# One token block of four taken alone through every mixer in plain float32, and two blocks instead of one served by gathered expert rows

## The chip, the cores and the metric

One core of a Trainium2 chip runs the whole kernel. The metric is the time of one execution on the device, in microseconds. Inputs and weights start in DRAM, the result ends there.

## What is computed

One layer over 512 tokens of 1024 channels, in float32. From the reference, cut:

```python
h = rmsnorm(x, norm_mix_g)
cb, cc, cx, q, k, v, gc, ga = split(h @ w_in)            # eight times 1024 columns
y_conv = (cb * causal_conv3(cc * cx)) @ w_conv_out
y_attn = diff_attention(q, k, v) @ w_attn_out            # 8 heads, causal, relative bias
x = x + (sigmoid(gc) * y_conv + sigmoid(ga) * y_attn) @ w_mix_out
x = x + cross_attention(rmsnorm(x), rmsnorm(mem))        # 256 memory positions, 4 heads
hf = rmsnorm(x)
# 8 heads each choose 16 of 16384 experts by two lists of 128 keys
act = gelu(einsum('td,thkd->thk', hf, peer_u[experts]))
x = x + einsum('thk,thkd->td', softmax(top_s) * act, peer_v[experts])
return rmsnorm(x, final_g)
```

## The kernel before

A block is 128 tokens. Up to the experts all four blocks (T = 512 columns) go together, channels on the partitions. A weight chunk of 1024 x 128 comes by one DMA of 512 KB on SP's queue (`weight`, line 106) and is split into two float32r parts, `hi` on ScalarE (line 98) and `lo` on VectorE (line 99), three buffers each. `product` (line 114) then makes 24 TensorE products: eight pieces of 128 channels, three passes each (hi by hi, hi by lo, lo by hi), 512 columns wide. There are 64 chunks of `w_in`, 8 each of four other mixers' weights and of `w_cq`, 16 of `w_pq`, and 16 of `w_ckv` (256 memory columns).

Order of the program: the memory's keys and values and the input's norm; eight heads of attention (`diff_head`), each beside one of eight convolution channels; the gates and the output projections; cross-attention; the queries and the choice of experts (`keys_scores`, `keys_pairs`); the experts. A scheduler orders each engine's instructions from this program; each engine then works in its own order.

The bias by distance is made once: `parameters` (line 192) lays a small table out and writes it, one copy per partition, to the DRAM tile `toep` by one DMA of 2560 KB from eight partitions; each head reads its part from there.

The experts are handled in two ways. Blocks 1 to 3 (TY = 384 columns, "dense") go against all experts: `stage_u` (line 687) multiplies 128 experts' chunk of `uT` with the dense tokens and applies gelu, 128 times; `gates` (line 823) lays the gates out densely with one-hot products, eight one-hot rows for four tokens; then for each of 128 chunks of `peer_v` 18 products of 512 columns sum up (line 750), six PSUM banks. The first 96 chunks of `uT` come before the first of `peer_v`, the other 32 beside them.

Block 0 is gathered: `gathered` (line 774) fetches, for step s below 128, one row of `peer_u` for each token by an indirect DMA issued by GpSimd, and VectorE multiplies it with the token's normed row and sums (line 801); for steps from 128 the same with `peer_v`, where VectorE adds the row times its weight to an accumulator (line 812). These 256 steps lie beside the dense work, from the choice of experts on. An index column is copied first (line 798).

The lines that the steps below touch most often:

```python
118             xhi, xlo = x[0][k], x[1][k]
119             for p, (ww, xx) in enumerate(((whi, xhi), (whi, xlo), (wlo, xhi))):
120                 self.nc.tensor.matmul(out, ww[:, k, :], xx, start=(k == 0 and p == 0), stop=(k == KC - 1 and p == 2))
...
801                     nc.vector.tensor_tensor_reduce(out=t, in0=t, in1=hx, op0=ALU.mult, op1=ALU.add, scale=1.0, scalar=0.0, accum_out=wx[:, 0, s : s + 1])
...
812                         nc.vector.scalar_tensor_tensor(out=acc, in0=t, scalar=w, in1=acc, op0=ALU.mult, op1=ALU.add)
...
818                 nc.gpsimd.indirect_dma_start(out=t, out_offset=None, in_=a["peer_u"] if s < P else a["peer_v"],
819                                              in_offset=bass.IndirectOffsetOnAxis(ap=idx, axis=0))
```

Of the kernel before, what the change touches and what calls it, by code (L numbers as in the profile page):

```python
# [32 lines left out]
NY = 3  # L33
# [11 lines left out]
SOON = 5  # memory weights loaded ahead of the input  # L45
# [6 lines left out]
MM = 1  # gate banks taken from the products  # L52
X_HEAD = 4  # gathered rows by two heads' choice
X_BLOCK = 3  # and by each block of tokens' gates
XW = 3  # rows in a step with an activation, to one in a step without
LAST = 2  # steps without rows at the end
LAST_J = 2  # blocks summed up token block by token block at the end
GRP = 8
TB = 24


class Block:
    # tag: (pool, slots)
    TAGS = {
# [22 lines left out]
    def ps(self, tag, shape=(P, 512)):  # L87
        self.count += 1
        return self.psum.tile(list(shape), F32, tag="ps" + tag, name=f"ps{tag}_{self.count}", bufs={"mm": 3, "lg": 2, "tr": 2, "pv": 1}[tag])

    def rows(self, name):
# [9 lines left out]
    def split_new(self, tag, src, n=T):  # L101
        hi, lo = self.t(tag, [P, n], F32R), self.t(tag, [P, n], F32R)
        self.split(hi, lo, src)
        return hi, lo

    def weight(self, dram_ap):
        raw = self.t("raw", [P, KC, P])
        self.nc.sync.dma_start(out=raw, in_=dram_ap)
        hi = self.t("hi", [P, KC, P], F32R)
        lo = self.t("lo", [P, KC, P], F32R)  # L110
        self.split(hi, lo, raw)
        return hi, lo

    def product(self, out, w, x):
        """out[c, t] = sum over d of w[d, c] x[d, t]"""
# [6 lines left out]
    def project(self, w, x, n=T):  # L122
        out = self.ps("mm")[:, :n]
        self.product(out, self.weight(w), x)
        return out

# [11 lines left out]
    def roots(self, out, acc, n, inv, eps, log=False, bank="tr"):  # L138
        """out[t, i] = 1 / sqrt(inv * sum of squares + eps) of token 128 i + t; acc holds sums by partition"""
# [26 lines left out]
    def spread(self, r, n, bank="tr"):  # L166
        """the tokens' values along the free dim, on every partition (in PSUM)"""
# [7 lines left out]
    def setup(self):  # L175
# [12 lines left out]
        m = self.misc = c("misc", [P, 48])  # L188
# [3 lines left out]
    def parameters(self):  # L192
        nc, a, m = self.nc, self.a, self.misc
        nc.vector.tensor_scalar(out=self.g_sub, in0=self.small[:, 56:57], scalar1=1.0 - LAM_INIT, scalar2=None, op0=ALU.mult)
        # lambda = exp(q1.k1) - exp(q2.k2) + init, the same on every partition
        lam = self.t("aw", [P, 4, 64])
        src = a["lam"]
        nc.gpsimd.dma_start(out=lam, in_=bass.AP(tensor=src.tensor, offset=src.offset, ap=[[0, P], [64, 4], [1, 64]]))
        for i in range(2):
            junk = self.t("aw", [P, 64])  # L200
# [4 lines left out]
        # relative bias by distance, reversed: entry e stands for distance 511 - e  # L205
        rb = self.t("vt", [32, H])
# [3 lines left out]
        oneh = [self.t("rs", [32, half]) for _ in range(2)]  # L210
        for i in range(2):
            nc.gpsimd.dma_start(out=oneh[i], in_=a["buckets"][:, i * half : (i + 1) * half])
        tab = self.t("aw", [H, TAB])
# [8 lines left out]
    def norm_of(self, x):  # L222
        acc = None
        for k in range(KC):
            acc = self.add_square(acc, x[k], T)
        r = self.misc[:, 8:12]
# [710 lines left out]
```

## Time and profile before

| what | value |
|---|---|
| median of 3 runs | 2156.46 us (2150.41 to 2160.2) |
| profiled execution, span | 2152.3 us |
| TensorE (PE) busy | 2048.0 us, 95% |
| VectorE (DVE) busy | 1505.0 us, 70% |
| ScalarE (ACT) busy | 1004.1 us, 47% |
| GpSimd (POOL) busy | 341.4 us, 16% |
| moved by DMA | 440.09 MB, mean 204 GB/s |

The profiled execution lies 4 us under the median and inside the range of the runs; its span is what the sums below are made against. PE, DVE, ACT, POOL and SP are the engines' names in the profile; PEld is TensorE's loading of weights. Products overlap in the profile (each lasts longer than the distance to the next one), so a rate is read from the distance between starts, not from the mean of one.

### The profile page before, as it was taken

The numbers are of one execution on the slowest core, as the hardware profiler recorded it, in microseconds if no ns is written. First come the engines' busy times: TensorE is split into PE (matmuls) and PEld (weight loads), VectorE is DVE, ScalarE is ACT, GpSimd is POOL, SyncE is SP. The second block draws the span as 40 slices with busy tenths as digits, with TensorE's granted clock in tenths as the row PEclk, the third lists the DMA queues.
The fourth block names the chain that finished last, engine by engine and source line by source line (L and its number), as shares of the span: only waits on it lengthen the run. The fifth ranks groups of instructions, "written<-read, shape, count | busy, mean of one in ns | idle before, by whom it ended". The sixth has DMA issues, their size and how long they took to land.

```text
span 2152.3 us, 29167 instructions
## 1 busy us (share of the span) xinstructions
PE 2048.0 (95%) x10341; PEld 1772.6 (82%) x10341; DVE 1505.0 (70%) x3531; ACT 1004.1 (47%) x1716; POOL 341.4 (16%) x301
## 2 busy tenths in 40 slices
PE   7499999999999999999998999999999999999997
PEld 6477877788887878899898989988777877888985
DVE  5356565642345568999887777557887887887897
ACT  5244444432233344343369999953333333333332
POOL 1000000000000000001231111012222234564431
PEclk9799999999999999999999999999999999999999
DMA  7532222223433124246687777589999988899984
GB/s 219 135 98 74 74 85 78 69 88 98 145 110 100 60 78 127 87 129 219 206 281 273 266 279 244 194 299 307 350 321 333 340 310 276 312 357 352 350 298 157
DMA packets 162787, 440.09 MB, mean 204 GB/s; under 512 B 15185, under 2 KB 70497, under 8 KB 160593
## 3 DMA queue, kind: packets, MB, share of 16 engines
q1 hardware_dynamic: 124464, 300.98, 41.7%
q0 software_dynamic: 38176, 137.25, 18.6%
q8 instruction: 81, 1.33, 0.2%
q14 instruction: 66, 0.53, 0.1%
HBM read 391.50 MB, written 46.66 MB: 204 GB/s over the span
## 4 chain that ended last, share of the span: by engine, by line
PE 51%; DMA 13%; DVE 13%; ACT 12%; issue 7%; POOL 2%; another core or an unknown queue 2%; SPq 0%; ACTq 0%; DVEq 0%; POOLq 0%
PE psmm L120 30%; PE psmm L750 5%; ACT slot L858 5%; PE pslg L120 5%; PE pstr L750 4%; DVE lo L99 3%; DMA raw<-in_peer_v 3%; DMA res<-in_peer_v,e 3%; ACT sq L850 3%; DMA act<-sp 2%; ACT hi L98 2%; PE pspv L750 2%; DMA res<-in_peer_u,e 1%; DMA res<-in_peer_u,kp 1%
## 5 line engine op out<-in xcount | busy, mean ns | idle before, releaser
L98 ACT ACTIVATE hi<-raw 128x1024 fp32r<-128x1024 f32 x388 | 410.9, 1061 | 633.0 <-PE psmm L120 288.4
L99 DVE TENSOR_TENSOR lo<-raw,hi 128x1024 fp32r<-128x1024 f32 x388 | 472.7, 1220 | 302.4 <-ACT hi L98 296.1
L120 PE MATMUL psmm<-A,hi 128*128 128x512 f32 x1408 | 451.1, 397 | 1.9 <-DVE Yb L450 1.9
L120 PE MATMUL psmm<-n,hi 128*128 128x384 f32 x1472 | 391.4, 343 | 1.2 <-ACT sp L695 1.2
L120 PEld LDWEIGHTS psmm<-A,hi 128*128 128x128 f32 x1408 | 262.3, 188 | 60.0 <-issue 4.2
L120 PE MATMUL psmm<-A,lo 128*128 128x512 f32 x704 | 280.6, 399 | 0.0
L120 PEld LDWEIGHTS psmm<-n,hi 128*128 128x128 f32 x1472 | 266.7, 188 | 1.6 <-ACT sp L695 1.5
L120 PE MATMUL psmm<-n,lo 128*128 128x384 f32 x736 | 251.6, 342 | 4.7 <-DVE lo L99 4.5
L818 POOL DMA_INDIRECT res<-in_peer_u,e x85 | 94.1, 1107 | 453.9 <-DVE e L798 430.2
L120 PEld LDWEIGHTS psmm<-A,lo 128*128 128x128 f32 x704 | 132.7, 189 | 28.6 <-issue 2.0
L98 ACT ACTIVATE tr<-e 128x384 fp32r<-128x384 f32 x128 | 66.6, 520 | 182.9 <-DVE e L739 179.0
L120 PE MATMUL pslg<-n,hi 128*128 128x384 f32 x576 | 148.3, 338 | 0.0
L120 PEld LDWEIGHTS psmm<-n,lo 128*128 128x128 f32 x736 | 138.3, 188 | 8.2 <-DVE lo L99 7.9
L750 PE MATMUL psmm<-hi,tr 128*128 128x512 f32 x384 | 129.0, 400 | 15.5 <-ACT tr L98 8.5
L801 DVE CUSTOM_DVE_ANT_0 res<-res,hx 128x1024 f32<-128x1024 f32 x101 | 122.5, 1219 | 24.8 <-DMA res<-in_peer_u,e 16.9
L750 PE MATMUL psmm<-lo,tr 128*128 128x512 f32 x384 | 131.1, 396 | 0.3 <-DVE lo L99 0.3
L818 POOL DMA_INDIRECT res<-in_peer_v,e x74 | 103.7, 1401 | 125.2 <-DVE e L808 103.1
L750 PE MATMUL psmm<-hi,e 128*128 128x512 f32 x384 | 119.6, 397 | 1.7 <-DVE e L798 1.6
L818 POOL DMA_INDIRECT res<-in_peer_u,kp x16 | 20.4, 1274 | 616.5 <-DVE kp L798 552.7
L120 PEld LDWEIGHTS pslg<-n,hi 128*128 128x128 f32 x576 | 105.3, 188 | 3.1
L856 DVE TENSOR_SCALAR oh<-iota,e 128x128 f32<-128x128 f32 x384 | 106.8, 345 | 0.0
L812 DVE SCALAR_TENSOR_TENSOR acc<-res,e,acc 128x1024 f32<-128x1024 f32 x73 | 93.5, 1281 | 15.8 <-DMA res<-in_peer_v,e 15.6
(299 smaller groups left out, 3748.2 us busy)
## 6 DMA issues: line engine op xcount, KB each, us to landing
raw<-in_uT SPq DMA_DIRECT2D x128, 512.0 KB, 4.5
raw<-in_peer_v SPq DMA_DIRECT2D x128, 512.0 KB, 5.9
raw<-in_w_in SPq DMA_DIRECT2D x64, 512.0 KB, 3.5
gates<-slot SPq DMA_DIRECT2D x16, 1536.0 KB, 6.7
slot<-gates SPq DMA_DIRECT2D x16, 1536.0 KB, 12.2
act<-sp SPq DMA_DIRECT2D x64, 192.0 KB, 3.8
raw<-in_w_pq SPq DMA_DIRECT2D x16, 512.0 KB, 3.5
raw<-in_w_ckv SPq DMA_DIRECT2D x12, 512.0 KB, 7.5
```

The lines of the kernel that those rows point to most:

```text
L98: self.nc.scalar.activation(hi, src, AF.Copy)
L99: self.nc.vector.tensor_tensor(out=lo, in0=src, in1=hi.bitcast(F32), op=ALU.subtract)
L120: self.nc.tensor.matmul(out, ww[:, k, :], xx, start=(k == 0 and p == 0), stop=(k == KC - 1 and p == 2))
L750: nc.tensor.matmul(accs[2 * i + half], l[:, ts], m[:, half * 512 : half * 512 + 512], start=(jj == 0 and p == 0), stop=(jj == NK - 1 and p ...
L801: nc.vector.tensor_tensor_reduce(out=t, in0=t, in1=hx, op0=ALU.mult, op1=ALU.add, scale=1.0, scalar=0.0, accum_out=wx[:, 0, s : s + 1])
L812: nc.vector.scalar_tensor_tensor(out=acc, in0=t, scalar=w, in1=acc, op0=ALU.mult, op1=ALU.add)
L818: nc.gpsimd.indirect_dma_start(out=t, out_offset=None, in_=a["peer_u"] if s < P else a["peer_v"], in_offset=bass.IndirectOffsetOnAxis(ap=i ...
L850: nc.scalar.activation(sq[:, w, :], self.iota, AF.Square, bias=it[:, t0 + w : t0 + w + 1], scale=-1.0)
L856: nc.vector.tensor_scalar(out=oh[:, 4 + w, :], in0=self.iota, scalar1=cols[:, 0, t - b * TB : t - b * TB + 1], scalar2=cols[:, 1, t - b * ...
L858: nc.scalar.copy(stage[:, :, q * 4 : q * 4 + 4].rearrange("p j w -> p w j"), pp.rearrange("p (w j) -> p w j", w=4))
```

## The change

Block 0 now goes first and alone through everything, from the norm to its choice of experts (`early`). Its products are plain float32, unsplit: 8 products of 128 columns for each of 120 weight chunks, which are loaded for it (`early_products`), four buffers; the same 120 chunks are loaded and split again for the other three blocks. Its keys, values and last two convolution inputs are kept for them. The other blocks' products are 384 columns wide instead of 512 (R). Their attention makes no query block 0.

The expert rows of block 0 (128 of `peer_u`, 128 of `peer_v`) are fetched from the second head on, spread over 110 calls of `weight` (START): 2.33 rows a call. `tick`, called by `weight` and in each `peer_v` step, copies an index into the tail of the weight's raw tile, issues the gather, and two calls later (WAIT) the row is used. There are five row buffers (`rw`).

Block 1, dense before, is gathered as well, over 250 calls from the choice of experts on (LAST). So two blocks are dense (TY = 256): `stage_u` has 256 columns, a `peer_v` step 12 products, the gates 256 tokens.

A `peer_u` row is used as before, by VectorE. A `peer_v` step now fetches the 128 rows of one token (by transposed indices), and TensorE sums over them: four plain float32 products, each with 32 weight columns of which one is not zero, 256 moving columns, and its own 32 partitions of one PSUM bank (`Rows.use`). PSUM goes from 3 banks for products to 2, with one for these sums. The bias of block 0 is read from `toep`.

```diff
-NY = 3
+NR = 3
+R = NR * P
+NY = 2
 TY = NY * P
...
-TB = 24
+TB = 16
+TAIL = 16
+WAIT = 2
+START = 110
+LAST = 250
...
+        "rw": ("q", 5),
+        "wz": ("z", 4), ...
...
     def weight(self, dram_ap):
-        raw = self.t("raw", [P, KC, P])
-        self.nc.sync.dma_start(out=raw, in_=dram_ap)
+        raw = self.t("raw", [P, KC * P + TAIL])
+        self.nc.sync.dma_start(out=raw[:, : KC * P], in_=dram_ap)
...
+        self.tick(raw[:, KC * P :])
...
-        for pair in range(2):
...
+        for qb in range(1, NT):
...
+    def early_products(self, ws, x, swap=False, bank="mm"):
+        nc = self.nc
+        out = self.ps(bank)
+        for i, src in enumerate(ws):
+            w = self.t("wz", [P, KC, P])
+            nc.sync.dma_start(out=w, in_=src)
+            for k in range(KC):
+                l, r = (x[:, k, :], w[:, k, :]) if swap else (w[:, k, :], x[:, k, :])
+                nc.tensor.matmul(out[:, i * P : (i + 1) * P], l, r, start=(k == 0), stop=(k == KC - 1))
+        return out.rearrange("p (c n) -> p c n", c=4)
...
+    def early(self):
...
+        nc.sync.dma_start(out=bias, in_=bass.AP(tensor=tp.tensor, ...
...
+        self.keys_gates(xe[2], r)
+        self.by_token(0, lambda c: x0[:, c, :], r)
+        return Rows(self, 0, xe, "ka")
...
+            first = self.early()
+            xT = self.load_x("x")
...
+                    if c == LAG:
+                        self.start_rows(first, START)
...
+            self.start_rows(Rows(self, 1, xe, "va"), LAST)
...
+    def tick(self, tail):
+        nc = self.nc
+        self.step += 1
+        while self.way and self.way[0][0] + WAIT <= self.step:
+            self.way.pop(0)[1]()
...
+        self.credit += self.rate
+        n = min(int(self.credit), self.nrows, len(self.todo))
+        self.credit -= n
+        idx = tail.bitcast(I32)
+        for k in range(n):
+            rows, s = self.todo.pop(0)
+            nc.vector.tensor_copy(idx[:, k : k + 1], rows.index(s))
+            t = self.row_tile()
+            nc.gpsimd.indirect_dma_start(out=t, out_offset=None, in_=self.a["peer_u" if s < P else "peer_v"],
+                                         in_offset=bass.IndirectOffsetOnAxis(ap=idx[:, k : k + 1], axis=0))
+            self.way.append((self.step, lambda rows=rows, s=s, t=t: rows.use(s, t)))
...
+class Rows:
...
+    def use(self, s, t):
+        b, nc, wx = self.b, self.b.nc, self.wx
+        if s < P:
+            nc.vector.tensor_tensor_reduce(out=t, in0=t, in1=self.hx, op0=ALU.mult, op1=ALU.add, scale=1.0, scalar=0.0, accum_out=wx[:, s : s + 1])
+            return
...
+        k, r = divmod(s - P, 32)
+        if r == 0:
+            nc.vector.tensor_copy(bass.AP(tensor=b.wd.tensor, offset=b.wd.offset, ap=[list(b.wd.ap[0]), [33, 32]]), self.wt[:, s - P : s - P + 32])
+            self.pv = b.ps("va")[:, :256]
+        for q in range(4):
+            nc.tensor.matmul(self.pv[32 * q : 32 * q + 32, :], b.wd[:, r, :], t[:, 256 * q : 256 * q + 256], start=(r == 0), stop=(r == 31))
+        if r == 31:
+            nc.scalar.copy(self.acc[:, k, :], self.pv)
```

Where instructions stand. First TensorE at the end of block 0, with the line numbers of the changed kernel: L412 are block 0's products, L576 its key scores, L1030 the transposed indices of its rows, L158 and L185 the norm of the other blocks, L134 their first product.

```order
L412 MATMUL psmm_2441<-zh_2148,wz_2474 128x128 x8
L576 MATMUL pslg_2483<-zv_2176,zl_2178 128x128 x4
L1030 MATMUL pstr_2603<-ident,wt_2600 128x128
L158 MATMUL pstr_2641<-ones,ss_2639 128x2 x3
L185 MATMUL pstr_2652<-ident,misc 128x128 x3
L281 MATMUL pstr_2831<-va_210,ident 128x128
L134 MATMUL psmm_2725<-A_2658,hi_2728 128x384
```

None of the other blocks' products stands ahead of the indices of block 0.

Then SP's queue early in the changed kernel: L409 are weight chunks of block 0, L120 chunks of the memory's weights, L452 the bias that is read from `toep`.

```order
L120 DMA raw_1035<-in_w_ckv 128x1024
L409 DMA wz_257<-in_w_in 128x1024
L409 DMA wz_267<-in_w_in 128x1024
L409 DMA wz_277<-in_w_in 128x1024
L409 DMA wz_287<-in_w_in 128x1024
L452 DMA z_212<-toep 128x8x128
L409 DMA wz_299<-in_w_in 128x1024
```

The bias read stands behind the first eight of the 120 chunks, and the others behind it.

Last, TensorE in a `peer_v` step of the changed kernel: L917 are the dense sums, L1056 the products of one gathered row.

```order
L917 MATMUL pstr_15555<-hi_18051,tr_18066 128x512
L1056 MATMUL psva_17515<-rw_18060,wd_90 32x256 x4
L917 MATMUL psmm_15552<-lo_18052,tr_18066 128x512
L917 MATMUL psmm_15553<-lo_18052,tr_18066 128x512
L917 MATMUL psmm_15552<-hi_18051,e_18067 128x512
```

Before, no such row stood on TensorE; now the 1024 of L1056 come in some 220 separate groups, most of four, between full-width products.

## Rows read from the trace of the kernel before

**Rows 1.** The page, part 1: busy time, share of the span, instructions of each engine.

```profile
PE 2048.0 (95%) x10341; PEld 1772.6 (82%) x10341; DVE 1505.0 (70%) x3531; ACT 1004.1 (47%) x1716; POOL 341.4 (16%) x301
```

**Rows 2.** Windows by stage: length, busy us (instructions) by engine, granted clock, DMA share, GB/s.

```profile
0.00:97.00 97.00, 53.52 (x359) 49.86 (x360) 39.63 (x75) 37.07 (x75) 6.68 (x18) 0.82 0.67 173
97.00:442.00 345.00, 345.00 (x1644) 272.93 (x1643) 215.21 (x489) 162.06 (x344) 5.90 (x27) 1.00 0.27 83
442.00:806.00 364.00, 359.69 (x1648) 296.70 (x1647) 170.97 (x261) 129.70 (x209) 0.00 (x0) 1.00 0.31 98
806.00:914.00 108.00, 108.00 (x572) 93.10 (x571) 101.07 (x520) 42.40 (x64) 0.00 (x0) 1.00 0.35 111
914.00:1425.00 511.00, 489.48 (x2971) 474.75 (x2971) 400.07 (x1190) 382.15 (x680) 74.58 (x64) 1.00 0.68 233
1425.00:2152.30 727.30, 692.36 (x3157) 585.30 (x3155) 578.04 (x1000) 250.69 (x346) 254.20 (x192) 0.98 0.89 314
```

**Rows 3.** Timeline of PE, start and us: float32r products of 512, 384, 256 columns.

```profile
302.34 0.39 PE L120 MATMUL psmm<-A,lo 128*128 128x512 f32 x1
...
305.74 0.39 PE L120 MATMUL psmm<-A,lo 128*128 128x512 f32 x1
...
930.35 0.34 PE L120 MATMUL psmm<-n,lo 128*128 128x384 f32 x1
...
935.13 0.34 PE L120 MATMUL psmm<-n,lo 128*128 128x384 f32 x1
...
22.57 0.28 PE L120 MATMUL psmm<-head,lo 128*128 128x256 f32 x1
...
25.05 0.28 PE L120 MATMUL psmm<-head,lo 128*128 128x256 f32 x1
```

**Rows 4.** Timeline of PE: plain float32 products back to back.

```profile
1304.33 1.05 PE L857 MATMUL psmm<-oh 128*128 128x128 f32 x8
...
17.39 0.70 PE L216 MATMUL pslg<-rs,vt 32*8 32x320 f32 x2
```

**Rows 5.** Source of L508, 64 plain float32 products: records, min/median/max ns, first and last start.

```profile
L508 PE MATMUL pslg<-sk,B x128: 270/275/276, 815.5 to 913.8; 128*128 128x128 f32 x128
```

**Rows 6.** DMA issues: count, KB each, median us to landing.

```profile
toep<-aw POOLq DMA_DIRECT2D x1, 2560.0 KB, 56.5
...
raw<-in_w_in SPq DMA_DIRECT2D x64, 512.0 KB, 3.5
...
res<-in_peer_v,e POOLq DMA_INDIRECT x74, 7.8
```

**Rows 7.** Windows early in the program, columns as in rows 2.

```profile
15.00:20.00 5.00, 5.00 (x39) 4.33 (x39) 3.98 (x8) 3.56 (x9) 0.77 (x2) 1.00 1.03 405
60.00:65.00 5.00, 0.00 (x0) 0.00 (x0) 0.00 (x0) 0.17 (x1) 0.00 (x0) 0.65 0.50 65
```

**Rows 8.** Source of L818, the first gathers: ns, first and last start.

```profile
L818 POOL DMA_INDIRECT res<-in_peer_u,kp x16: 936/939/3568, 964.0 to 1047.3; - x16
```

**Rows 9.** Groups of DVE by form: count, busy us, mean ns, idle before.

```profile
L99 DVE TENSOR_TENSOR lo<-raw,hi 128x1024 fp32r<-128x1024 f32 x388 | 472.7, 1220 | 302.4 <-ACT hi L98 296.1
...
L801 DVE CUSTOM_DVE_ANT_0 res<-res,hx 128x1024 f32<-128x1024 f32 x101 | 122.5, 1219 | 24.8 <-DMA res<-in_peer_u,e 16.9
...
L798 DVE COPY e<-ex 128x1 int32<-128x1 int32 x93 | 14.0, 150 | 7.4 <-DMA res<-in_peer_v,e 2.2 <-DMA oh<-in_peer_v,e 1.3 <-PE pspv L750 1.0
...
L856 DVE TENSOR_SCALAR oh<-iota,e 128x128 f32<-128x128 f32 x384 | 106.8, 345 | 0.0
```

**Rows 10.** Timeline of PE at 126 us: a product on 64 of the 128 rows.

```profile
126.26 0.28 PE L282 MATMUL pslg<-head,head 128*128 128x256 f32 x1
...
126.47 0.39 PE L283 MATMUL pslg<-head,head 64*128 64x256 f32 x1
...
126.78 0.50 PE L120 MATMUL psmm<-A,lo 128*128 128x512 f32 x1
```

More of the change, by code (lines that the diff above doesn't have):

```diff
@@ L209, in parameters @@
         half = TAB // 2
-        oneh = [self.t("rs", [32, half]) for _ in range(2)]
+        oneh = [self.t("zs", [32, half]) for _ in range(2)]
         for i in range(2):
             nc.gpsimd.dma_start(out=oneh[i], in_=a["buckets"][:, i * half : (i + 1) * half])
-        tab = self.t("aw", [H, TAB])
+        tab = self.t("z", [H, TAB])
         for i in range(2):
@@ L254, in diff_head @@
             nc.vector.scalar_tensor_tensor(out=q[other[c]], in0=pp[own[c]], scalar=0.125, in1=q[own[c]].bitcast(F32), op0=ALU.mult, op1=ALU.subtract)
[L255 removed]
+        pp = self.ps("mm")
+        nc.tensor.matmul(pp[:, :P], self.ident, self.k0[:, h, :], start=True, stop=True)
+        self.product(pp[:, P:], self.weight(a["w_in"][32 + h]), x)
         for c, k in enumerate(ks2):
@@ L314, in diff_head @@
+        po = self.ps("pv")[:, :R]
+        for k in (0, 2, 3, 1):
+            ks, q0 = slice(k * P, (k + 1) * P), max(k - 1, 0) * P
+            for p, (v, w) in enumerate(((vhi, ahi), (vhi, alo), (vlo, ahi))):
+                nc.tensor.matmul(po[:, q0:], v[:, ks], w[:, k, q0:], start=(k == 0 and p == 0), stop=(k == 1 and p == 2))
+        raw, sq = self.t("rs", [P, R]), self.t("rs", [P, R])
         nc.scalar.copy(raw, po)
         nc.scalar.activation(sq, raw, AF.Square)
-        r = self.t("rh", [P, NT])
@@ new lines, in early_roots @@
+    def early_roots(self, out, src, ni, inv, eps, log=False, bank="pv"):
+        nc = self.nc
+        ss = self.ps(bank)
+        sqs = []
+        for t, k0 in src:
+            sq = self.t("z", [P, 4, ni * P])
+            nc.scalar.activation(sq, t[:, k0 : k0 + 4, :], AF.Square)
+            sqs += [sq[:, k, :] for k in range(4)]
+        for i in range(ni):
+            for k, sq in enumerate(sqs):
+                nc.tensor.matmul(ss[:, 2 * i : 2 * i + 2], sq[:, i * P : (i + 1) * P], self.ones[:, 0:2], start=(k == 0), stop=(k == len(sqs) - 1))
+        self.inverse_root(out, ss[:, : 2 * ni].rearrange("p (i o) -> p i o", o=2)[:, :, 0], inv, eps, log)
@@ L586, in tokens @@
         at, y = [], []
-        with left("att") as self.pools["h"]:
-            self.pools["r"] = right.enter_context(self.sb("input", "right"))
-            mem = self.memory()
-            xT = self.load_x("x")
-            self.parameters()
-            rb = self.norm_of(xT)
-            self.memory_products(*mem)
-            h = self.normed(xT, self.g_mix, rb)
-            right.close()
-            self.pools["r"] = right.enter_context(self.sb("conv", "right"))
+        self.pools["g"] = self.rest.enter_context(self.sb("kept", "right"))
+        self.pools["r"] = right.enter_context(self.sb("input", "right"))
+        self.wd = self.t("wd", [P, 32, 32])
+        nc.gpsimd.memset(self.wd, 0.0)
+        with left("early") as self.pools["z"]:
+            self.pools["x"] = self.pools["z"]
+            first = self.early()
+            xT = self.load_x("x")
+            rb = self.norm_of(xT)
+            h = self.normed(xT, self.g_mix, rb)
+        right.close()
+        for p in "bq":
+            self.pools[p] = self.rest.enter_context(self.sb(p, "right"))
+        self.pools["r"] = right.enter_context(self.sb("conv", "right"))
+        with left("att") as self.pools["h"]:
             for c in range(KC + LAG):
@@ L640, in tokens @@
         self.e = [self.t("e", [P, NY, H, TOPK]) for _ in range(3)]
-        self.xe = [self.t("xe", [P, 1, H, TOPK]) for _ in range(3)]
-        self.by_token(xT, rtok)
+        assert len(self.todo) <= P and not any(s < P for _, s in self.todo)
+        xe = [self.t("xe", [P, 1, H, TOPK]) for _ in range(3)]
+        for i in range(1, NT):
+            self.by_token(i, lambda c: xT[c][:, (i - 1) * P : i * P], rtok[:, i - 1 : i])
         with left("keys") as self.pools["x"]:
@@ L716, in experts @@
         self.stages(PROLOGUE)
-        accs = [self.ps(tag) for tag in ("mm", "mm", "mm", "tr", "tr", "pv")]
+        accs = [self.ps(tag) for tag in ("mm", "mm", "tr", "tr")]
         vtab = a["peer_v"].rearrange("(i j) d -> j i d", j=NK)
         gt = None
-        left = 2 * P - self.rows_done
-        sums = np.cumsum([XW if PROLOGUE - AHEAD <= j < NK - AHEAD else 1 for j in range(NK - LAST)])
-        ends = [int(np.ceil(left * c / sums[-1])) for c in sums] + [left] * LAST
         ready = []
@@ L752, in experts @@
                 ready = []
-            self.gather.send(ends[j] - (ends[j - 1] if j else 0))
+        self.flush()
+        fin = self.misc[:, 24:27]
+        for rows in self.sets:
+            rows.out()
         fg = self.t("hx", [P, D])
-        nc.sync.dma_start(out=fg, in_=self.rows("final_g"))
-        fin = self.misc[:, 24:28]
-        for i in range(NT):
-            xt = [self.t("B") for _ in range(2)]
+        nc.sync.dma_start(out=fg, in_=self.rows_of("final_g"))
+        for i in range(NT - NY, NT):
+            xt = [self.t("z1") for _ in range(2)]
             y = self.t("hi" if i % 2 else "lo", [P, D])
+            k = i - (NT - NY)
             for half in range(2):
@@ new lines, in start_rows @@
+    def start_rows(self, rows, steps):
+        self.sets.append(rows)
+        self.todo += [(rows, s) for s in range(2 * P)]
+        self.rate = len(self.todo) / steps
+    def tick(self, tail):
+        nc = self.nc
+        self.step += 1
+        while self.way and self.way[0][0] + WAIT <= self.step:
+            self.way.pop(0)[1]()
+        if not self.todo:
+            self.credit = 0.0
+            return
[10 more added lines that the diff above has]
+            self.way.append((self.step, lambda rows=rows, s=s, t=t: rows.use(s, t)))
@@ L823, in gates, with flush @@
+    def flush(self):
+        assert not self.todo
+        while self.way:
+            self.way.pop(0)[1]()
     def gates(self, ei, ej, eg):
```

580 lines of the change are left out of this document (340 added, 240 removed), and 14 rows, old and new, of the table TAGS.

## Prediction, made before the changed kernel was timed

> **What bounds the kernel now.** I read the busy shares first: TensorE is busy 95% of the span, VectorE 70% [rows 1]. An average hides where that changes, so I cut the span into six stages at the first or last instruction of a line: A, input and memory (to 97 us); B, attention and convolution (to 442); C, gates, projections, cross-attention (to 806); D, queries and scores (to 914); E, activations of the first 96 blocks of experts and the dense gates (to 1425); F, the sums over experts and the output [rows 2]. The reader is to see that PE is at or near its full time from B to F, and that VectorE is next: 101 of 108 us in D, 400 of 511 in E, but only 215 of 345 in B. In A neither is: PE works 54 of 97 us. So the change is worth what it takes from PE, stage by stage, until VectorE or a new wait ends the stage.
>
> **What it takes from PE.** Distances between starts: 512 columns, fifteen products in 3.40 us, 0.227 each; 384 columns, 27 in 4.78, 0.177; 256 columns, 21 in 2.48, 0.118 [rows 3]. That is proportional to the columns, so narrower products are not held up by their weight loads. The mixers' and queries' 2880 products save 0.050 each, 143 us; the 3072 of the activations 0.059, 181; 768 of the 2304 in the sums over experts go, 174. With some 25 us of one-hot products, scores and attention of one block it is about 520 us.
>
> **What it adds, A.** Block 0 needs 960 plain float32 products. Eight records of 128 columns take 1.05 us with the last one's 0.28, so 0.110 from one to the next [rows 4], and 64 such products in the program left 128 records [rows 5]: two records, 0.22 us, each. 960 x 0.22 = 211 us. The memory's products stay, 384 x 0.118 = 45; attention, scores and transposes of block 0 are some 20: 276 us of PE. Three waits come on top. First, the bias table's write: 56.5 us to landing, where a weight chunk takes 3.5 [rows 6]; while it ran, the DMA moved 65 GB/s against 405 before [rows 7]. The bias read now waits for it in SP's queue, and 112 of the 120 chunks stand behind that read. I let the write start near 28 us, as before, and the queue go on at 84 us; PE has then done 28 us of work, so the rest ends at 84 + 248 = 332. Second, about 18 us where PE waits for norms and the softmax of cross-attention, some ten VectorE operations of 0.7 us or less on each path (an estimate). Third, the choice of experts: from the last score to the first gather took 50 us before (913.8 to 964.0) [rows 5, 8]. Here three quarters of it lie beside the query products; the ends are 0 and 50, I take 30, since two of the four groups' sorting is left and the other blocks' products stand behind the index transpose on PE. A then ends at 380, **283 later**.
>
> **B.** PE falls to 345 - 57 - 6 = 282. VectorE becomes the bound. Its 215 us hold 48 splits of 1.22 us [rows 9], 59, unchanged; the other 156 shrink with the columns to some 125. New are the rows: 42 of the calls lie here, at 2.33 a call 98 `peer_u` rows, each 1.22 + 0.08 (its sum read out) + 0.15 (the index copy) [rows 9]: 142. Sum 326, with some waits 335: **10 less**, not 63.
>
> **C.** PE: 364 - 67 (56 chunks) - 10 = 287. The last 30 `peer_u` rows make VectorE the slower one for 13 calls, some 20 us. Then 100 `peer_v` rows come on PE. **D:** PE 79 without rows, plus 28 rows; VectorE 77. **E:** VectorE's 400 us lose a third of the one-hot work (107 us [rows 9] and 27 of its smaller group), 45, and some 23 of sorting, and gain 98 - 64 rows x 1.45 = 49: 381 us. PE needs only 330. I take 410, the share of waits that such a bound leaves: **101 less**. **F:** 727 - 174 - 45 = 508, and 128 `peer_v` rows on PE. The transfers there, some 190 MB, would take 605 us at the 314 GB/s of this stage [rows 2] and 545 at 350: just beside the rest.
>
> **The price of a row on PE**, p, decides. Without rows the stages are 380 + 335 + 307 + 79 + 410 + 508 = 2019 us; so span = 2019 + 256 p. A row is four products of 256 columns, two records each of 256 / 128 x 0.110 = 0.22 us. Two records on one place of the array ran one after the other (0.70 us for two of 320 columns, 0.27 apart, which is their full length) [rows 4]. So the upper end is eight in a row, 1.76; the lower end is all four quarters beside each other, 0.44. I take the middle case: the second record of a quarter waits for its first, and the first of the next quarter, on other columns of the array, goes beside it: five lengths, 1.10. Changing the array's shape also costs: a product on 64 rows started 0.21 after its forerunner and held the next one 0.31, where 0.118 each was due, 0.28 for a visit [rows 10]; some 220 visits are 62 us, 0.24 a row. p = 1.34, 343 us, less some 20 us in which PE idles in F anyway (727 - 692 [rows 2]): **2342 us of span**. VectorE would have paid 1.28 us for such a row; that work goes there, but VectorE is not the bound in C and F.
>
> Fetching costs little: 512 gathers instead of 256, each some 1.3 us of POOL beside other work; 134 MB more of rows and 63 MB of weights loaded twice lie in stages that moved 83 to 111 GB/s [rows 2], except E and F.
>
> The profiled run lies 4 us under the median: **2346 us** forecast.
>
> **Rivals.** *First, all four quarters run together*, the change of shape hidden as well: p = 0.44, in C, D and F. 2019 + 113 = 2132, with the 4 us 2136, **faster** by 0.9%. It decides from p = 0.52 down. For it: the four have their own columns and their own PSUM partitions; against it: rows 4 and 10. The Trainium skill (TensorE: Matmul & The Clock Gate, Part 3: Packing small matmuls) says that products in different column groups of the array run concurrently, and gives 2.38 times for three; no run here shows it, and by that rule this rival is right. The skill's other page on it (TensorEngine Tiling (Array Packing), Key Properties) says that a change of tiling mode drains the engine; the 0.28 us of rows 10 agree, and by that rule the 62 us of visits stay and this rival's sum is 2194, slower too. *Second, nothing overlaps*: p = 1.76 + 0.24 = 2.0, 2531 + 4 = 2535. For it: the in-order pairs; against it: nothing but that the quarters are apart. *Third, the rows come late, so that the change does not fetch them beside the mixers' work*: landing takes 7.8 us [rows 6], there are five buffers, and a row is held to its use; if use follows after some 3 us, five rows take 1.3 + 7.8 + 3 = 12 us, 2.4 a row, against 3.4 in B and 2.9 in C. It would bind if landing went to some 14 us: about 100 us more, 2450.
>
> **Chances.** Forecast 0.46, first rival 0.27, second 0.17, third 0.10. The forecast's own range is 2260 to 2430: A may end 25 us earlier or later, E is bounded by 381 and 440, p by a fifth of it. The range over all, 2105 to 2530, leaves out the lower quarter of the first rival and half of the second. About 0.5% can be told from no change here, 2146 to 2167: faster has two thirds of the first rival and a little of the forecast's tail, 0.21; between, 0.07; slower 0.72.
>
> **What would show it.** In the changed profile the first 384-column product should start near 380 us, with PE idle between 45 and 84 us and for some 30 us at the end of A. In B VectorE should be busy over 93% and PE under 90%. The first of the four products of a row and the next row's first, back to back, should start some 0.9 to 1.1 us apart: near 0.45 is the first rival, 1.8 the second. In F a step should take near 4.2 us. If PE waits for row transfers by more than some 20 us in all, the third rival is at work. The forecast is wrong in its signs if A ends before 330 us or p is under 0.5.

## The result, and the profile after

The changed kernel takes 2401.97 us (median of 4 runs, 2398.35 to 2405.98), the kernel before 2158.33 beside it: 1.114 times as long (95% interval 1.111 to 1.118). **Slower**, by 244 us. The forecast was 2346, with a range of 2105 to 2530. The profiled run has a span of 2396.6 us.

The page's busy times by engine, to be read against [rows 1]:

```profile
PE 2021.7 (84%) x13374; PEld 1732.7 (72%) x13374; DVE 1461.3 (61%) x3810; ACT 889.6 (37%) x1549; POOL 596.1 (25%) x526
```

PE works 26 us less than before, in a span that is 244 us longer. So the question is not what PE was given to do, but where it stands still. The windows by stage of the changed kernel, cut at the same instructions as [rows 2] and with its columns:

```profile
0.00:423.00 423.00, 329.79 (x2612) 321.44 (x2613) 133.23 (x414) 71.83 (x131) 6.58 (x14) 0.89 0.67 209
423.00:812.00 389.00, 314.63 (x1586) 284.67 (x1586) 330.40 (x768) 161.79 (x297) 135.99 (x116) 0.88 0.67 228
812.00:1166.00 354.00, 334.16 (x2257) 276.98 (x2258) 167.35 (x390) 116.39 (x198) 115.32 (x113) 0.96 0.72 253
1166.00:1280.00 114.00, 107.28 (x787) 91.03 (x786) 87.90 (x440) 37.73 (x68) 26.87 (x28) 0.97 0.71 235
1280.00:1762.00 482.00, 358.15 (x2732) 345.80 (x2731) 383.41 (x1097) 270.30 (x517) 128.51 (x99) 0.89 0.78 267
1762.00:2396.60 634.60, 577.70 (x3408) 412.78 (x3406) 359.04 (x705) 231.59 (x340) 182.84 (x158) 0.96 0.89 307
```

| stage | before | forecast, with p = 1.34 | after | after less forecast |
|---|---|---|---|---|
| A, input, memory, block 0 alone | 97 | 380 | 423 | +43 |
| B, attention and convolution | 345 | 335 | 389 | +54 |
| C, gates to cross-attention | 364 | 441 | 354 | -87 |
| D, queries and scores | 108 | 117 | 114 | -3 |
| E, activations and gates | 511 | 410 | 482 | +72 |
| F, sums and output | 727 | 660 | 635 | -25 |
| span | 2152 | 2342 | 2397 | +54 |

The sum came within 55 us, its terms did not: C and F are cheaper than forecast, A, B and E dearer. The readings below show why.

**The rows on PE are cheap.** PE's timeline in C: start, duration, operation, count of records.

```profile
904.95 0.34 PE L134 MATMUL psmm<-B,lo 128*128 128x384 f32 x1
905.22 1.07 PE L1056 MATMUL psva<-rw,wd 128*32 128x256 f32 x16
906.22 0.62 PE L134 MATMUL psmm<-A,hi 128*128 128x384 f32 x2
...
906.93 0.64 PE L1056 MATMUL psva<-rw,wd 128*32 128x256 f32 x8
907.50 0.44 PE L134 MATMUL psmm<-A,hi 128*128 128x384 f32 x1
```

Sixteen records are two rows of four products, two records each; 1.00 us after their start the next mixer product starts. Eight records, one row, hold the next product back for 0.57 us. A further row in the same visit thus costs 0.43 us, two record lengths of 0.22, where eight such lengths lie in it. In F each row comes alone, between products of 512 columns:

```profile
2055.08 0.62 PE L917 MATMUL pstr<-lo,tr 128*128 128x512 f32 x2
2055.54 0.63 PE L917 MATMUL pstr<-hi,e 128*128 128x512 f32 x2
2056.10 0.64 PE L1056 MATMUL psva<-rw,wd 128*32 128x256 f32 x8
2056.67 0.73 PE L917 MATMUL psmm<-hi,tr 128*128 128x512 f32 x2
2057.23 0.63 PE L917 MATMUL pstr<-hi,tr 128*128 128x512 f32 x2
```

Two such products take 0.46 us otherwise (2055.08 to 2055.54); with the row after them it is 1.13 (2055.54 to 2056.67), 0.67 more, and the pair after it takes 0.10 too long: some 0.76 us for a lone row.

**In B VectorE has what the forecast gave it** (330 us of work; 326 were forecast, though with 98 `peer_u` rows and not the 114 that ran here), but it also waits. Its two largest groups of B: count, busy us, mean ns, and idle time before them with its releaser.

```profile
L1041 DVE CUSTOM_DVE_ANT_0 rw<-rw,hx 128x1024 f32<-128x1024 f32 x114 | 138.7, 1220 | 32.3 <-DMA rw<-in_peer_u,raw 32.0
L111 DVE TENSOR_TENSOR lo<-raw,hi 128x1024 fp32r<-128x1024 f32 x50 | 60.9, 1218 | 5.3 <-ACT hi L110 4.5 <-PE psmm L134 0.9
```

32 us are waits for rows that had not landed. Yet the rows landed 5.6 us after their issue (median of B), sooner than the 7.8 us that the forecast reckoned with [rows 6].

**In E PE waits, though no engine is full** (PE 358 us of 482, VectorE 383). PE's two longest waits there (what waited, for what; us, times, longest), then ScalarE's from 1310 us:

```profile
PE psmm L134 <- ACT sp L865: 50.1, 24, 13.7
PE pstr L1030 <- DVE wt L1027: 23.3, 1, 23.3
```

```profile
ACT hi L110 <- DMA raw<-in_uT: 62.7, 21, 25.4
...
ACT sp L865 <- DMA act<-sp: 50.0, 25, 5.2
```

`sp` is the one buffer from which the activations of chunks 32 to 95 are written to DRAM. PE waits for a PSUM bank, gelu (the `sp` of L865) holds the bank, and gelu waits until an earlier result has left its one buffer. None of the prediction's steps has this wait.

### The profile page after: what moved, and what is told of

Read it like the earlier page. It is cut to its first block, busy times and chain, and to the rows that moved or that the text cites. A ratio compares the mean times of both kernels' runs of the same rounds, so it can differ in the third digit from the quotient of the medians.

```text
span 2396.6 us, 36423 instructions
## 1 busy us (share of the span) xinstructions
PE 2021.7 (84%) x13374; PEld 1732.7 (72%) x13374; DVE 1461.3 (61%) x3810; ACT 889.6 (37%) x1549; POOL 596.1 (25%) x526
## 4 chain that ended last, share of the span: by engine, by line
PE 46%; DMA 19%; DVE 13%; issue 11%; ACT 6%; POOL 2%; another core or an unknown queue 2%; SPq 1%; ACTq 0%; DVEq 0%; POOLq 0%
PE psmm L134 14%; PE psmm L412 8%; DMA rw<-in_peer_u,raw 8%; PE psmm L917 6%; PE pstr L917 5%; PE psva L1056 5%; PE pslg L134 4%; DVE rw L1041 3%; DVE lo L111 3%; DMA rw<-in_peer_v,raw 2%; DMA raw<-in_peer_v 2%; ACT hi L110 2%; DMA act<-sp 2%; POOL rw L970 2%
## 5 line engine op out<-in xcount | busy, mean ns | idle before, releaser
L970 POOL DMA_INDIRECT rw<-in_peer_u,raw x256 | 319.4, 1248 | 1140.6 <-DVE raw L968 472.9
L970 POOL DMA_INDIRECT rw<-in_peer_v,raw x256 | 270.1, 1055 | 583.3 <-PE psva L1056 241.9
L134 PE MATMUL psmm<-A,hi 128*128 128x384 f32 x1408 | 392.8, 358 | 25.9 <-DVE hq L269 9.0
L1041 DVE CUSTOM_DVE_ANT_0 rw<-rw,hx 128x1024 f32<-128x1024 f32 x256 | 311.6, 1220 | 91.8 <-DMA rw<-in_peer_u,raw 91.4
L134 PE MATMUL psmm<-n,hi 128*128 128x256 f32 x1472 | 290.9, 299 | 76.1 <-ACT sp L865 50.1
L134 PEld LDWEIGHTS psmm<-n,hi 128*128 128x128 f32 x1472 | 243.0, 203 | 84.0 <-ACT sp L865 55.3
L134 PEld LDWEIGHTS psmm<-A,hi 128*128 128x128 f32 x1408 | 266.4, 200 | 50.1 <-issue 23.4
L134 PE MATMUL psmm<-A,lo 128*128 128x384 f32 x704 | 247.5, 352 | 0.3 <-DVE raw L968 0.3
L134 PE MATMUL psmm<-n,lo 128*128 128x256 f32 x736 | 214.5, 293 | 0.7 <-DVE raw L968 0.4
L412 PE MATMUL psmm<-zh,wz 128*128 128x128 f32 x1280 | 163.4, 292 | 41.0 <-DMA wz<-in_w_in 40.6
L412 PEld LDWEIGHTS psmm<-zh,wz 128*128 128x128 f32 x1280 | 159.6, 208 | 43.9 <-DMA wz<-in_w_in 31.1
L1056 PE MATMUL psva<-rw,wd 128*32 128x256 f32 x2048 | 173.1, 392 | 3.5 <-ACT ka L1058 2.7
L134 PEld LDWEIGHTS psmm<-n,lo 128*128 128x128 f32 x736 | 148.6, 203 | 1.1 <-DVE lo L111 1.1
L134 PEld LDWEIGHTS psmm<-A,lo 128*128 128x128 f32 x704 | 139.9, 199 | 1.9 <-issue 1.2
L917 PE MATMUL psmm<-hi,tr 128*128 128x512 f32 x256 | 88.0, 426 | 30.1 <-ACT hi L110 30.0
L1056 PEld LDWEIGHTS psva<-rw,wd 128*32 128x32 f32 x2048 | 52.8, 109 | 77.3 <-issue 55.1
L134 PE MATMUL pslg<-n,hi 128*128 128x256 f32 x576 | 107.6, 286 | 1.0 <-ACT hi L110 1.0
L134 PEld LDWEIGHTS pslg<-n,hi 128*128 128x128 f32 x576 | 89.6, 191 | 12.3 <-issue 8.2
```

The source lines that it names most:

```text
L412: nc.tensor.matmul(out[:, i * P : (i + 1) * P], l, r, start=(k == 0), stop=(k == KC - 1))
L917: nc.tensor.matmul(accs[2 * i + half], l[:, ts], m[:, half * 512 : half * 512 + 512], start=(jj == 0 and p == 0), stop=(jj == NK - 1 and p ...
L970: nc.gpsimd.indirect_dma_start(out=t, out_offset=None, in_=self.a["peer_u" if s < P else "peer_v"], in_offset=bass.IndirectOffsetOnAxis(ap ...
L1041: nc.vector.tensor_tensor_reduce(out=t, in0=t, in1=self.hx, op0=ALU.mult, op1=ALU.add, scale=1.0, scalar=0.0, accum_out=wx[:, s : s + 1])
L1056: nc.tensor.matmul(self.pv[32 * q : 32 * q + 32, :], b.wd[:, r, :], t[:, 256 * q : 256 * q + 256], start=(r == 0), stop=(r == 31))
```

## The experiments

All kernels are edits of the changed kernel (2402 us, span 2397), but for one, which is an edit of the kernel before. A time without a range is that of one execution; the kernel before took 2154 to 2158 us on the same chips. Where there are several runs, the ratio has its interval. Stages are cut at the same instructions as above.

### One column group for all four quarters

```diff
-nc.tensor.matmul(self.pv[32 * q : 32 * q + 32, :], ...)
+nc.tensor.matmul(self.pv[:32, :], ...)
...
```

> All four products of a peer_v row write the same 32 PSUM partitions, so they use the same 32 columns of the array (the sums of block 0's and block 1's peer_v rows then mix their quarters; same number of products, same sizes). Theory 1, the changed kernel's trace read as full overlap (0.43 us for each further row of a visit, 0.57 for a lone one): the eight records now follow one another at 0.22, 1.76 a row, so 1.33 more for each of 256 rows, 340 us of PE; C and D, where PE is busy 94%, grow by some 170, F by some 120 to 170, since PE has about 57 idle there: about 2690 us in all (2640 to 2740). Theory 2, the forecast's half overlap (1.10 a row): 0.66 more a row, about 2570. Theory 3, no overlap before either: no change, 2400.

Measured: 2646.9 us. PE's timeline in C:

```profile
1088.07 5.37 PE L1056 MATMUL psva<-rw,wd 128*32 128x256 f32 x24
1093.37 0.62 PE L134 MATMUL psmm<-Y,hi 128*128 128x384 f32 x2
```

Three rows now take 5.30 us, 1.77 each: eight record lengths of 0.22, one after the other. In the changed kernel the same products take 0.43. So the four quarters do run beside each other, all four of them, and the second theory, the forecast's half overlap, falls with the third. By stages C grew by 98 us, D by 33 and F by 145, and E became 25 shorter; the whole grew by 245. That lies in theory 1's range; C and D, which hold 128 rows, grew by 131 and not by its 170.

### The row sums left out

```diff
-for q in range(4):
-    nc.tensor.matmul(self.pv[32 * q : 32 * q + 32, :], b.wd[:, r, :], ...)
...
```

> The products of the peer_v rows are left out (the rows are still fetched, and the sum over them is zero). Theory 1 (a row costs 0.43 us and a visit some 0.25 to 0.3 beside it): C falls by about 104 x 0.7 = 73 us to 280, D by 15, F by at most 50, because its transfers (90% of the DMA engines' time) then end it: about 2265 us (2240 to 2300). Theory 2, the forecast's 1.34 a row: 343 us of PE go, C would fall by 139 to 215, the whole to some 2080 to 2150.

Measured: 2302.2 us. C's window:

```profile
821.00:1118.00 297.00, 267.88 (x1488) 258.28 (x1489) 168.19 (x401) 114.58 (x196) 130.93 (x123) 0.95 0.85 318
```

C falls from 354 to 297: 57 us for its 96 rows (768 records of L1056 lie in C, not the 104 rows of the expectation), 0.59 a row. The timeline gives nearly that for two rows in a visit: from 904.95 to 906.22 less one product's 0.18, by two, 0.55. 1.34 is out. D falls by 25 for its 32 rows, F by only 27, of some 97 us that its 128 lone rows cost PE: another limit is close behind PE there; the run without the gathers, next, points to the transfers. The whole fell by 100 and not by 137; F's part was sized too large.

### The gathers left out

```diff
-t = self.row_tile()
-nc.gpsimd.indirect_dma_start(out=t, ...)
+t = self.still
```

> The 512 gathers are left out (every use reads one still row of zeros; index copies, multiplications and products stay). Theory late rows: VectorE loses the waits on peer_u rows that the changed trace shows (about 32 us in B, 44 in E, 9 in F) and F's transfers no longer hold it: B falls from 389 to about 350, E from 482 to about 430, F from 635 to about 570, the whole to about 2230 us (2190 to 2280). Theory work alone (VectorE's and PE's instructions are the bound, the transfers hidden): B and E within 10 us of the changed kernel's, the whole over 2370.

Measured: 2242.5 us, so 159 us go with the row transfers. B's window:

```profile
429.00:792.00 363.00, 310.25 (x1582) 281.43 (x1583) 337.01 (x784) 162.89 (x300) 0.00 (x0) 0.88 0.23 74
```

B falls by 26, C by 23, D by 14, E by 35, F by 64. VectorE is now busy 337 of B's 363 us. So the row transfers cost some 26 us in B. The third rival's condition is not met, though: the rows land in 5.6 to 7.1 us in all stages and not in 14, and by its own sign PE would wait over 20 us for rows, where the changed trace has 2. It is VectorE that waits for `peer_u` rows: 32 us in B, 6 in C, 44 in E and 9 in F. Why they come too late for it was not tested. The larger part of the 159 us is F, where the transfers and PE are about equally long.

### The bias on its own queue, then the table written from 128 partitions

```diff
-nc.sync.dma_start(out=bias, in_=bass.AP(tensor=tp.tensor, ...
+nc.gpsimd.dma_start(out=bias, in_=bass.AP(tensor=tp.tensor, ...
```

> Block 0's read of the bias goes on GpSimd's queue, right behind the table's write, instead of SP's; all else in the same order. Theory queue (the forecast's term: the 112 chunks behind the read wait for the write): weight chunks go on coming from 28 us, PE's idle 32 us between 28 and 84 go, A ends 25 to 40 us earlier, the whole is about 2370 us. Rival: the write itself holds the DMA engines (85 GB/s moved in that time), so the chunks come no earlier: A within 10 us, 2395 to 2405.

Measured: 2379.7 us; A ended 10 us earlier. PE was busy 23.7 us between 28 and 84, as without the edit (23.8), and over A it waited 35 us for chunks of `w_in` (41 without it). SP's queue had indeed stood 36 us before the bias read (46.8 to 83.1), but with that wait gone the chunks came hardly sooner: seven in place of four were issued between 30 and 80 us, and they took 32.1 us to land. So the queue was at most 10 us of A. Of the whole's 22 us another 9 lie in E, which this edit does not touch; with one run they stay open. The DMA issues of the changed kernel between 30 and 80 us (queue, packets, MB, share of 16 engines; then KB each and median us to landing) show what delays the chunks:

```profile
q0 software_dynamic: 1009, 2.51, 44.7%
q1 hardware_dynamic: 576, 2.10, 13.0%
...
wz<-in_w_in SPq DMA_DIRECT2D x4, 512.0 KB, 33.9
```

The table's write (q0) takes 54.5 us to land and holds 45% of the engines' time meanwhile, and the weight chunks beside it land after 33.9 us, where the median from 84 us on is 4.4. The next run writes the same bytes from all partitions:

```diff
-pt = self.ps("lg")[:H, :half]
-nc.tensor.matmul(pt, rb, oneh[i], start=True, stop=True)
...
-nc.gpsimd.dma_start(out=self.toep, in_=tab.rearrange("h (o e) -> h o e", o=1).to_broadcast([H, P, TAB]))
+for h in range(H):
...
+        nc.tensor.matmul(pt, rb[:, h : h + 1].to_broadcast([32, P]), oneh[i][:, :n], start=True, stop=True)
...
+    nc.gpsimd.dma_start(out=self.toep[h], in_=tab)
```

> The bias table's 2560 KB are written by eight DMAs of 320 KB from 128 partitions each (TensorE lays each head's row on all partitions, 16 products instead of 2) in place of one DMA from eight partitions. Theory: the one write is slow because it leaves from eight partitions, and holds the DMA engines; spread out it takes some 10 us in all, PE's idle 32 us between 28 and 84 us go, A falls from 423 to about 390 us, the whole to about 2370 (2355 to 2380). Rival: the write costs by its bytes and its place in the queue, or other chains hold A: A within 10 us of 423, the whole over 2385.

Measured: 2353.4 us. The window from 28 to 84 us:

```profile
28.00:84.00 56.00, 55.61 (x414) 49.50 (x414) 9.52 (x23) 7.61 (x16) 4.36 (x8) 1.00 0.76 256
```

PE is busy 55.6 of 56 us (23.8 before), the DMA moves 256 GB/s (85 before), A ends at 388: 35 us earlier. The whole gained 48. In the first 100 us q0 moves 3.01 MB in both kernels; that took 25.8% of the engines' time and takes 9.6% now. The Trainium skill (DMA: Bandwidth & Descriptors, Rules for kernel authors) says that an outermost dimension smaller than 16 confines a DMA to at most that many of its engines; the table's eight heads were the outermost dimension, and the trace agrees: the DMA share was 0.54 in that window of the changed kernel, and 0.50 at 60 us in the kernel before [rows 7]. That rule would halve the engines; it does not give the 25.8% against 9.6%. The edit changes the number of engines, the source partitions and the number of DMAs together, and which of them makes each byte cost less was not separated.

The same edit in the kernel before, where PE waited for chunks beside the same write:

> The kernel before, with the bias table written from 128 partitions as above and nothing else changed. Theory: PE's 36 us of waits for weight chunks in the first 97 us, which lie beside the slow write, go for the most part: 2120 to 2135 us, faster than both kernels by 1 to 2%. Rival: the write is not what delays the chunks: 2148 to 2162.

Measured: 2128.85 us (2125.9 to 2135.3), 0.989 of the kernel before (0.985 to 0.992). Its windows:

```profile
28.00:60.00 32.00, 31.63 (x204) 25.19 (x202) 22.59 (x51) 15.24 (x30) 4.00 (x8) 1.00 0.73 243
60.00:97.00 37.00, 36.80 (x215) 31.80 (x215) 16.83 (x21) 18.50 (x39) 1.30 (x5) 1.00 0.48 158
```

PE is full from 28 us on, where the kernel before had it busy 21 us of the first window and 13 of the second. This version takes less time than either kernel.

### The transposed indices made later

```diff
-pt = b.ps("tr")[:, :P]
-nc.tensor.transpose(pt, exf, b.ident)
-nc.vector.tensor_copy(self.ext, pt)
...
 def index(self, s):
+    if s == P:
+        pt = b.ps("tr" if self.block == 0 else "pv")[:, :P]
+        nc.tensor.transpose(pt, self.exf, b.ident)
+        nc.vector.tensor_copy(self.ext, pt)
```

> The transposed expert indices of a gathered block, which only the peer_v rows read, are made when the first of those is fetched, not right after the choice of experts. Theory order: PE stood 25 us at the end of A and 23 us at the start of E before that one transpose, with the other blocks' products behind it; they now go ahead: A 20 to 25 us shorter, E some 20 shorter, the whole 2355 to 2370 us. Rival: VectorE's sorting is what everything there waits for, so what PE gains it loses in the next stage: the whole over 2385.

Measured: 2389.1 us. The other blocks' products start at 399 us, 24 earlier, but B ends at the same time (813): it has become 414 us long. E is 6 shorter, though PE's wait before the second such transpose had been 23 us. The rival holds for A: at the end of A the sorting of block 0's experts on VectorE is what counts, and PE only waited in another place.

### The multiplications of the `peer_u` rows left out

```diff
-nc.vector.tensor_tensor_reduce(out=t, in0=t, in1=self.hx, ..., accum_out=wx[:, s : s + 1])
```

> VectorE's 256 multiplications of peer_u rows by the normed tokens are left out (the rows are still fetched, their sums are zero). Theory VectorE bound (the forecast's for B and E): B loses 148 us of VectorE's 330 and 30 of its waits and falls from 389 to 325 to 335, where PE's 315 busy hold it; E falls from 482 to about 425; C and D stay; F stays within 15: the whole about 2285 us (2260 to 2310). Rival: the attention's chain of waits holds B, whatever VectorE has beside it: B stays over 370, the whole over 2350.

Measured: 2278.1 us. B's window:

```profile
428.00:722.00 294.00, 285.02 (x1582) 262.37 (x1582) 206.28 (x538) 160.66 (x295) 112.79 (x112) 0.98 0.81 287
```

B falls by 95 us to 294, with the gathers still there, and PE is busy 97% of it: VectorE's work on the rows bounds B. It falls further than expected because PE needs only 285 us, the forecast's 282; the 315 in the changed kernel are the same products at a mean granted clock of 0.88 in place of 0.98. E lost only 18 us of the 57 expected: in E the rows on VectorE are not the main thing.

### Index tiles of their own

```diff
-idx = tail.bitcast(I32)
+idx = self.t("ix", [P, TAIL]).bitcast(I32)
```

> The index columns of the gathers go into six small tiles of their own instead of the tails of the weight chunks' three raw tiles; nothing else changes. Theory coupling: a raw tile is held until the gathers that read their indices from its tail are through, so the next weight chunk's load waits for a row's buffer (the changed trace: SP's queue waits 138 us in E for the transfers of peer_u rows, 36 times, the longest 44, and ScalarE 63 us there for uT chunks); without it E falls from 482 to 430 to 450, B from 389 to 370 to 380, the whole to about 2340 us (2315 to 2360). Rival: the chunks are late only because VectorE, which splits them, is: E within 10 us, the whole over 2380.

Measured: 2399.8 us, no change, and not for the rival's reason. B became 422 us, C 332, E 585, F 530. E's window and VectorE's rows there:

```profile
1282.00:1868.00 586.00, 443.17 (x3398) 389.40 (x3396) 422.97 (x1264) 274.44 (x520) 275.30 (x218) 0.88 0.90 325
```

```profile
L1041 DVE CUSTOM_DVE_ANT_0 rw<-rw,hx 128x1024 f32<-128x1024 f32 x128 | 155.0, 1212 | 3.2 <-DMA rw<-in_peer_u,ix 3.1
```

The scheduler's order changed with the edit, and the rows came earlier: all 128 `peer_u` rows and 90 of the `peer_v` rows of block 1 lie in E (98 and none in the changed kernel). Waits for `peer_u` rows in E went from 44 to 3 us, but the DMA is busy 90% of E. E and F together are 1116 us in both kernels: rows can be moved between the stages without gain. VectorE now waits 74 us in E for buffers of `peer_v` rows instead. My theory falls; since the order moved too, what the coupling by itself costs stays open.

### Three spill buffers, and edits together

```diff
-"sp": ("d", 1)
+"sp": ("d", 3)
```

> Three buffers instead of one for the activations that are written out to DRAM between gelu and the sums over experts. Theory spill: PE waits 50 us in E for a PSUM bank that gelu holds while its one buffer is still being written out (ScalarE waits 50 us for those writes); with three buffers E falls from 482 to 435 to 450, the whole to about 2365 us (2350 to 2375). Rival: PE would wait for the next chunk or for VectorE instead: E within 10 us, the whole over 2385.

Measured: 2340.9 us. E's window, and what is left of PE's wait there:

```profile
1285.00:1714.00 429.00, 340.89 (x2719) 328.80 (x2718) 374.24 (x1076) 267.94 (x518) 128.24 (x98) 0.92 0.86 297
```

```profile
PE psmm L134 <- ACT sp L865: 4.0, 7, 1.0
```

E falls from 482 to 430, PE's wait behind gelu from 50 us to 4, and VectorE's waits for rows there from 44 to 5 us as well. One buffer of 1 KB per partition was worth 52 of the 72 us by which E exceeds its forecast. With the table:

> The changed kernel with the two edits that each gave time alone: the bias table from 128 partitions (A 35 us shorter, the whole 48) and three spill buffers (E 53 shorter, the whole 61). If they add up, 2293 us (2280 to 2305), and the kernel with all four edits (2272) owes 20 us to the index tiles and the late transpose. If they share a bound, 2310 to 2335.

Measured: 2291.2 us (2287.8 to 2291.4), 1.063 of the kernel before (1.060 to 1.066): the two gains add up. All four edits:

> The changed kernel with four of the edits together: the bias table written from 128 partitions, the late transpose of the indices, index tiles of their own, three spill buffers. If the waits are separate, the gains add up: 44 us (measured, table) + 8 (measured, transpose) + 60 (own index) + 35 (spills) = 147: about 2255 us (2225 to 2290), still 4 to 5% slower than the kernel before. If they share one bound (VectorE in B and E), the own index and the spills give little more than one of them: 2300 to 2340. Below 2158 would need that the whole early stage is hidden, which nothing here does.

Measured: 2272.4 us (2269.5 to 2291.5), 1.058 of the kernel before (1.052 to 1.063). A is 369, B 425, C 336, E 433: of what A and C win, B loses 36 us, as it lost with the late transpose and the index tiles alone. Those two edits, 13 and 2 us alone, give 19 here. The four edits together are worth 130 us of the 244. The other 114 were not taken apart; A alone is still 272 us longer than before. Beside the kernel before with its table written the same way (2129), these four edits leave the change 143 us slower.

## Why the prediction came out

**Right.** The sign and its main reason: what E and F give back is less than A costs. A alone grew by 326 us (283 forecast); B to D together lost another 40 (76 forecast), E and F gave back 122 (168 forecast). Where B to D lose came out otherwise: B, forecast 10 shorter, grew by 44, and C, forecast 77 longer, lost 10. The cadences held: block 0's products at 0.22 us each where the granted clock was 1.00 (16 in 3.58 us at 125.81), VectorE's work in B (330 us for 326, with more rows and less else), PE's 282 in B (285 without the rows' multiplications), the queue going on at 84 us (the bias read was issued at 83.1), 30 us for the tail of the choice of experts (33: from the last score at 390 to 423).

**Wrong: the price of a row on PE.** The step "the second record of a quarter waits for its first, and the first of the next quarter goes beside it: five lengths, 1.10" is false. All four quarters run together, 0.43 us a further row, as the first rival said; one column group takes 1.77. Of that rival's two halves only this one held: the change of shape still costs some 0.2 to 0.3 us a visit, so a row comes to 0.55 in pairs and 0.76 alone, some 0.65 in the mean. 256 x (1.34 - 0.65) = 177 us too dear. By the rule on packing in the Trainium skill (TensorE: Matmul & The Clock Gate, Part 3) the quarters run concurrently, and the trace agrees (1.77 by 0.43 is 4.1). By the Trainium skill's other page (TensorEngine Tiling (Array Packing), Key Properties), on the drain between tiling modes, the rival's sum was 2194; the 0.2 to 0.3 us of these visits agree with it. I put rows 4, two records on one place of the array, above the rule that spoke of different places, and rows 4 could not tell of those.

**Wrong the other way, by as much.** With p = 0.65 the formula 2019 + 256 p gives 2185; the span is 2397. The missing 212 us lie in the terms below; C, at 354 for 307 + 96 x 0.55 = 360, is 6 under.

- E, "I take 410, the share of waits that such a bound leaves": too low by 72. 52 are the one spill buffer, which in the kernel before, with longer products, cost little (ScalarE waited 14 us for it there, PE 1). PE's wait before the index transpose of block 1, 23 us, is in the rest, but moving it gave only 6; the other 14 stay open. The step looked at what PE and VectorE do in E, not at what else has a fixed time per chunk when the chunk gets shorter.
- B, "sum 326, with some waits 335": VectorE's sum was right (with 16 rows more and some 20 us less of other work), the waits were 59 us and not 9. 32 are waits for rows, with rows that landed faster than the forecast's 7.8 us; without the gathers B takes 363. The forecast's sign, VectorE busy over 93% of B, failed: 85%.
- A, 43 over: PE's work was put at 276 us and is 330. Block 0's products hold PE 236 us and not 211, at a mean granted clock of 0.89 over A, the memory's 49 (45), the rest 45 and not 20. Of this PE has done 39 us by 84 us, and not 28, so 291 are left there and not 248: the 43. The waits behind 84 us are 48, as forecast (18 and 30). The write's price was right too: PE was to be idle between 45 and 84 us, 39 us, and with the write spread out A is 35 shorter. But the step "the bias read waits in SP's queue" named the wrong main cause: the write holds the DMA engines, so the chunks are late on any queue, and without the wait in the queue A ended only 10 us earlier. That the price fits is luck.
- F: 508 + 128 x 0.76 = 605, measured 635. "Just beside the rest" was 30 us short: without the gathers F takes 570, without the row products 607.
- D: 79 + 32 x 0.6 = 98, measured 114; without the row products it takes 89. Its rows thus cost 0.8 each there, and 10 us come from elsewhere, not tested further.

The forecast time is close by luck: two errors of about 200 us, 177 too much and 212 too little, offset each other, and the 20 us of idle that the forecast took off make up the rest of the 55. The stages, not the sum, show that. Of the signs that I named, the distance between rows (0.43) pointed to the first rival, and still the kernel is slower: the rival's time on the faster side also needed the stages without rows to come out as forecast, and the change of shape to cost nothing.

## What to carry to other kernels

When a change shortens a loop's main work, list everything in the loop that has a fixed time per turn (a write out of a single buffer, a landing time, a sort) and ask whether it fits into the shorter turn. Moving transfers to a quiet stage pays only if the engine that consumes them has room in that stage, and a second pass over all weights (A, 326 us here) must be paid by what it removes elsewhere, which was 82 us here. Look at what a slow transfer does to its neighbours before looking at who waits for it in a queue.

## What was not expected of the hardware

- Plain float32 products of 32 columns on four column groups overlap fully, although each is two records: four in 0.43 us, 1.77 on one group.
- A single DMA of 2560 KB from eight partitions took 54.5 us; while it ran, 512 KB chunks from another queue took 33.9 us to land in place of 4.4.
- The granted clock was lower over the stages where PE stood still in between: 0.88 over B (PE busy 315 of 389 us) and 0.89 over E (358 of 482), against 1.00 over both in the kernel before (345 of 345, 489 of 511). Windows of 4 us in B, columns as in rows 2:

```profile
500.00:504.00 4.00, 4.00 (x27) 3.96 (x25) 3.97 (x7) 1.36 (x3) 1.34 (x2) 1.00 0.88 286
504.00:508.00 4.00, 0.98 (x3) 0.37 (x2) 3.26 (x9) 3.36 (x5) 2.27 (x2) 0.77 0.92 302
508.00:512.00 4.00, 0.00 (x0) 0.00 (x0) 2.12 (x9) 1.32 (x5) 2.15 (x2) 0.50 0.92 279
512.00:516.00 4.00, 1.46 (x7) 1.46 (x8) 2.82 (x7) 0.00 (x0) 0.00 (x0) 0.50 0.76 293
516.00:520.00 4.00, 3.20 (x13) 2.81 (x13) 4.00 (x9) 2.12 (x5) 0.00 (x0) 0.50 0.00 0
520.00:524.00 4.00, 4.00 (x16) 4.00 (x15) 3.55 (x9) 0.86 (x2) 0.00 (x0) 0.59 0.24 66
524.00:528.00 4.00, 4.00 (x22) 3.40 (x22) 2.65 (x7) 3.17 (x7) 0.00 (x0) 1.00 0.02 4
```

  PE stands still from about 505 us and is granted 1.2 GHz (0.50 of the full 2.4) through the work that follows, up to some 523; only then does it run at 2.4 GHz again. B's products took 315 us of PE so, and not the 285 of the run without the rows' multiplications. In B VectorE set the end and not PE; what the lower clock costs in E was not measured.
